# Strassen's seven products for the GLA values of a hybrid attention block

## The chip, the cores and the metric

The kernel runs on one core of one Trainium2 chip. The time is device microseconds of one execution, from its start to its last store. TensorE multiplies, VectorE and ScalarE do the elementwise work, GpSimd helps and issues some DMAs, SyncE issues most of the others.

## The reference

One layer of an encoder block on x (1 × 512 tokens × 2048, float32). What matters here:

```python
mod = silu(c) @ w_cond + b_cond
shift, scale, gate = split(mod, 3)
h = rms_norm(x) * (1 + scale) + shift
aq, ak, av, ag, gq, gk, gv, gg, lr_f, lr_b = split(h @ w_in)   # 1024 x4, 512, 512, 1024, 1024, 16, 16
a_out = dilated_attention(aq, ak, av) * silu(ag)               # 16 heads of 64, 3 patterns
log_g = log_sigmoid(lr @ gla_gate_up + bias) / 16              # forward and backward
g_out = rms_norm(gla(gq, gk, gv, log_g_f) + gla_backward(...)) * gain * silu(gg)   # 4 heads
y = concat(a_out, g_out) @ w_out
return rms_norm(x + gate * y) * final_gain
```

`gv = h @ W` is a product of 512 tokens × 2048 by 2048 × 1024. It is needed by all four GLA heads.

## The kernel before

**Precision.** Each float32 operand is split into a high part (ScalarE rounds it, `split_hi`) and the rest (VectorE subtracts, `split_lo`); a product is three matmuls, high by high, low by high and high by low (`three`, L217 to L219). `h_hi` and `h_lo` hold h transposed, 16 tiles of 128 features by 512 tokens.

**Units.** After the conditioning sums and two first units, the projection goes through units of 512 output columns: `qk2`, `qk4`, `qk6`, `gk`, `gv0`, `gv1`, `ag0`, `ag1`, `gg0`, `gg1`. A unit reads 8 weight groups of 512 KB (two tiles of 128 × 512), and each group takes 24 matmuls into four PSUM tiles. `fetch` loads a group on SyncE's queue, some groups ahead, into a pool of four buffers (`RAW`); the high and low parts have three buffers each. Then the output projection follows as two pairs of column blocks, each by Strassen's seven products (`OUT_ORDER`): four groups of 12 matmuls a product, `O0` to `O55`. Sums of weight blocks for it (T1 to T4) are made in memory by copies and accumulating DMAs on GpSimd's queue (`paced`, L393), spread over the units by `SUM_OPS_IN`; its sums of `cat` (S1 to S4) are made by VectorE.

**Side work.** A unit takes a list of (share, function): at that share of its ticks the function's instructions are issued. In the units `qk2` to `gk` this is the attention of 16 heads, four a unit: scores `s` by TensorE, an exponential `p` with its sum (VectorE and ScalarE, L736 and L739), a reciprocal (L740), a multiply by GpSimd (L744), transposes `t` (L756), an addition into `pt` (L761) and the product `o` (L770). In `gv1`, `ag0`, `ag1` and `gg0` it is one GLA head each, `gla_head`: gate logits `z` for two directions (`z00`, `z01` for head 0), then on ScalarE and VectorE their log-sigmoid `g`, its running sum `b`, a shifted copy `bm`, and the decayed `ki` and `qi`; TensorE transposes `ki` (`kt00`, `kt01`), multiplies with the values (`kv`), and so on. `SUMS_IN` spreads conditioning sums (`rawv`, `rawg`, VectorE, L316) over the units.

**The values.** `gv0` and `gv1` are such units with h as the stationary and the weights as the moving operand, so that the tokens lie on the partitions of the result. The low-rank gate input `plr` (32 matmuls) lies in `gv0`; between the two units it is stacked (`lrst`), the gate's up-projection `ups` is loaded and split; GLA head 0 starts at a fifth of `gv1` (`GLA_FIRST`).

**What sets the order.** TensorE's instructions stay in the order in which the program writes them. The other engines' are ordered by a scheduler's priorities; `urgent` raises those of side work, `issue_after(last["lo"])` puts an operation behind the last low split in VectorE's order, and `paced` ties a DMA to the last high split.

## Time and profile before

| | |
|---|---|
| median of three runs | 930.07 us (929.69 to 930.33) |
| profiled execution | 930.08 us, span 928.3 us |
| TensorE busy | 914.6 us (99%), granted clock 1.0 in every stage but the last (0.96) |
| VectorE, ScalarE, GpSimd busy | 654.9, 472.1, 100.7 us |
| DMA | 210.84 MB, mean 227 GB/s |

The stages by TensorE's time, read off the timeline:

| stage | us from the start |
|---|---|
| conditioning and first units | 0 to 188 |
| qk2, qk4, qk6, gk, with the attention | 188, 255, 321, 387 to 453 |
| gv0, with the low-rank matmuls | 453.3 to 507 |
| gv1, with GLA head 0 | 507 to 559.7 |
| ag0, ag1, gg0 with heads 1 to 3, gg1 | 559.7, 613, 667, 721 to 772 |
| output projection and tail | 772 to 928 |

In a row of the timeline the first two numbers are start and duration in us; square brackets hold the idle time of the engine before it and what ended that. A row of the table of windows gives the busy time of each engine between two times, the number of instructions in brackets, then the granted clock, the share of the DMA engines and GB/s. Matmuls overlap, so the distance of two starts, and not the duration, tells what one costs.

### The profile page before, as it was taken

The numbers are of one execution on the slowest core, as the hardware profiler recorded it, in microseconds if no ns is written. First come the engines' busy times: TensorE is split into PE (matmuls) and PEld (weight loads), VectorE is DVE, ScalarE is ACT, GpSimd is POOL, SyncE is SP. The second block draws the span as 40 slices with busy tenths as digits, with TensorE's granted clock in tenths as the row PEclk, the third lists the DMA queues.
The fourth block names the chain that finished last, engine by engine and source line by source line (L and its number), as shares of the span: only waits on it lengthen the run. The fifth ranks groups of instructions, "written<-read, shape, count | busy, mean of one in ns | idle before, by whom it ended". The sixth has DMA issues, their size and how long they took to land.

```text
span 928.3 us, 12115 instructions
## 1 busy us (share of the span) xinstructions
PE 914.6 (99%) x4375; PEld 759.6 (82%) x4375; DVE 654.9 (71%) x960; ACT 472.1 (51%) x770; POOL 100.7 (11%) x152
## 2 busy tenths in 40 slices
PE   8999999999999999999999999999999999999995
PEld 6888788888888888888877888888888888888884
DVE  7988799866665766767544747576696539697496
ACT  5553533565654655655513545364553338455564
POOL 0000000012212223122000110101021000000001
PEclk9999999999999999999999999999999999999998
DMA  9999497564765775655665647668686667856743
GB/s 347 403 414 387 161 378 294 182 210 134 193 198 156 208 237 155 219 167 172 186 235 192 187 137 243 199 203 252 210 266 193 207 176 269 315 183 230 280 171 136
DMA packets 54629, 210.84 MB, mean 227 GB/s; under 512 B 7237, under 2 KB 7525, under 8 KB 46249
## 3 DMA queue, kind: packets, MB, share of 16 engines
q1 hardware_dynamic: 48946, 175.89, 51.9%
q0 software_dynamic: 5184, 33.62, 15.4%
q8 instruction: 34, 0.56, 0.2%
q10 hardware_dynamic: 440, 0.57, 0.2%
q14 instruction: 25, 0.20, 0.1%
HBM read 201.57 MB, written 37.84 MB: 258 GB/s over the span
## 4 chain that ended last, share of the span: by engine, by line
PE 92%; DVE 3%; ACT 2%; DMA 1%; issue 1%; SPq 0%; DVEq 0%; ACTq 0%
PE ps_qk L217 5%; PE ps_qk L219 5%; PE ps_qk L218 5%; PE g L219 4%; PE g L217 4%; PE g L218 4%; PE o L770 3%; PE ps_gv L219 3%; PE ps_gv L218 3%; PE stb L219 3%; PE ps_gv L217 3%; PE stb L217 3%; PE stb L218 3%; PE t L756 3%; PE ps_ag L217 3%; PE ps_ag L219 3%
## 5 line engine op out<-in xcount | busy, mean ns | idle before, releaser
L316 DVE CUSTOM_DVE_ANT_0 cb<-cb,sb,c_bcond 128x2048 f32<-128x2048 f32 (+1 forms) x32 | 73.4, 2295 | 1.6 <-DMA cb<-in_wm 1.2
L739 ACT ACTIVATE p<-p,st 128x512 f32<-128x512 f32 x64 | 46.1, 721 | 53.1 <-DVE st L736 52.6
L393 POOL DMA_DIRECT2D T<-in_w_o x48 | 33.5, 704 | 305.5 <-ACT qk21h L444 119.8
L744 POOL TENSOR_SCALAR p<-p,st 128x512 f32<-128x512 f32 x62 | 44.6, 719 | 194.7 <-DVE st L740 141.5
L736 DVE CUSTOM_DVE_ANT_0 p<-s,g 128x512 f32<-128x512 f32 x64 | 43.7, 687 | 18.0 <-PE s L733 17.7
L761 DVE TENSOR_TENSOR pt<-t,pt 128x512 fp32r<-128x512 f32 x64 | 43.7, 688 | 15.0 <-ACT pt L760 14.7
L760 ACT ACTIVATE pt<-t 128x512 fp32r<-128x512 f32 x64 | 37.8, 591 | 11.1 <-PE t L756 10.0
L756 PEld LDWEIGHTS t<-c_ident,p 128*128 128x128 f32 x256 | 31.5, 140 | 9.7 <-POOL p L744 1.4
L756 PE MATMUL t<-c_ident,p 128*128 128x128 f32 x256 | 38.5, 273 | 0.1
L770 PEld LDWEIGHTS o<-pt,vv 128*128 128x128 f32 x256 | 34.8, 188 | 2.8
L770 PE MATMUL o<-pt,vv 128*128 128x256 f32 x256 | 35.6, 281 | 0.0
L740 DVE RECIPROCAL st<-st 128x1 f32<-128x1 f32 x64 | 10.3, 161 | 24.5 <-ACT p L739 24.4
L733 PE MATMUL s<-kl,qs 128*128 128x512 f32 x64 | 25.0, 391 | 0.0
L732 PE MATMUL s<-ks,qs 128*128 128x512 f32 x64 | 25.0, 390 | 0.0
L945 ACT ACTIVATE sq<-st,sc 128x256 f32<-128x256 f32 x24 | 12.2, 507 | 19.7 <-DVE st L935 10.5
L777 DVE TENSOR_TENSOR cat<-o,oh 64x256 f32<-64x256 f32 x32 | 13.3, 417 | 11.1 <-ACT oh L773 10.7
L1273 POOL TENSOR_SCALAR x<-x,rn 128x512 f32<-128x512 f32 x3 | 3.4, 1132 | 158.4 <-ACT rn L1262 158.4
L316 DVE CUSTOM_DVE_ANT_0 rawg<-rawg,crow,c_bcond 128x1024 f32<-128x1024 f32 x16 | 20.4, 1279 | 0.0
L316 DVE CUSTOM_DVE_ANT_0 rawg<-rawg,crow,gate 128x1024 f32<-128x1024 f32 x16 | 20.2, 1278 | 0.2 <-DMA rawg<-in_wg 0.2
L773 ACT ACTIVATE oh<-o 64x256 f32<-64x256 f32 x32 | 12.2, 381 | 15.0 <-PE o L770 14.0
L508 ACT ACTIVATE h_hi<-xt,shift 128x512 fp32r<-128x512 f32 x16 | 11.5, 719 | 12.8 <-DVE shift L316 12.8
L977 PE MATMUL go<-qi,sq 128*128 128x128 f32 x96 | 15.9, 275 | 0.0
(1520 smaller groups left out, 2968.1 us busy)
## 6 DMA issues: line engine op xcount, KB each, us to landing
cb<-in_wm SPq DMA_DIRECT2D x31, 1024.0 KB, 8.5
T<-in_w_o POOLq DMA_DIRECT2D x48, 512.0 KB, 5.2
rawg<-in_wg SPq DMA_DIRECT2D x32, 512.0 KB, 4.8
raw_O<-T SPq DMA_DIRECT2D x32, 512.0 KB, 4.5
raw_qk<-in_w_qk SPq DMA_DIRECT2D x24, 512.0 KB, 3.4
raw_O<-in_w_o SPq DMA_DIRECT2D x24, 512.0 KB, 3.3
rawb<-in_w_sb SPq DMA_DIRECT2D x16, 512.0 KB, 5.3
rawv<-in_wv SPq DMA_DIRECT2D x16, 512.0 KB, 3.4
```

Source lines behind the costliest of these rows:

```text
L217: mm(ps, lh, rh, start=first, stop=False, skip_group_check=more)
L218: mm(ps, ll, rh, start=False, stop=False, skip_group_check=more)
L219: mm(ps, lh, rl, start=False, stop=last, skip_group_check=more)
L316: nc.vector.tensor_tensor_reduce(out=w, in0=w, in1=with_, op0=ALU.mult, op1=ALU.add, scale=1.0, scalar=init, accum_out=dst)
L393: move = nc.gpsimd.dma_start(dst, src, max_dma_last_dim=8192, **how).ins
L736: nc.vector.tensor_tensor_reduce(out=t, in0=ps, in1=gt[h][:, P * i:P * i + 512], op0=ALU.add, op1=ALU.min, scale=1.0, scalar=3e38, accum_o ...
L739: act(t, t, AF.Exp, bias=st[:, 0:1], scale=-1.0, accum_out=st[:, 1:2])
L744: last["pool"] = nc.gpsimd.tensor_scalar(t, t, st[:, 2:3], 1.0, op0=ALU.mult, op1=ALU.mult).ins
L756: nc.tensor.transpose(pk[:, kt * P:kt * P + P], t[:, kt * P:kt * P + P], ident)
L760: act(hi, src, AF.Copy)
L761: tt(lo, src, hi.bitcast(F32), op=ALU.subtract)
L770: mm(po[:, :256], vv[h // 4][:, kt, h % 4, :], t[:, w, kt, :], start=kt == 0 and w == 0, stop=kt == 3 and w == 1)
```

## The change

`gv0` and `gv1` become one unit `V` of seven products (`VAL_ORDER`), in blocks of 256 tokens and 1024 features by 1024 features and 512 columns. Each product has four groups of 12 matmuls, `V0` to `V27`: 336 instead of 384.

- Its token sums S1 to S4 are made by VectorE in the units qk2, qk4, qk6 and gk (`token_sums`: three operations on 128 × 512 at 0.3 of the unit's ticks, seven at 0.75), stored to memory on SyncE's queue in pieces of 256 KB, loaded again in `V` (eight loads of 512 KB) and split there (`vS...`).
- Its weight sums T1 to T4 are made in memory on GpSimd's queue, 32 operations. The output projection's T1 no longer is (16 operations less): its two blocks are loaded (`raw_O`, `raw_P`) and added by VectorE (L471).
- P2, P4, P5 and P3 are merged into `gv0` and `gv1` by VectorE (L1280, L1282 and others) as their PSUM is read.
- In `V` the low-rank matmuls come at ticks 10 to 40, the gate's preparation (`up_load`, `up_split`, `lr_stack`) is side work, and GLA head 0 gets shares of its own (`GLA_FIRST`).
- Conditioning sums move out of the value units: `SUMS_IN` gives qk4 5, qk6 5, gk 6, ag0 8, ag1 8, gg0 9, and the rest (7) fall to gg1.

```diff
 GLA_AT = (0.01, 0.02, 0.33, 0.46, 0.46, 0.56, 0.64, 0.76, 0.76, 0.88)
-GLA_FIRST = 0.2
-
-SUMS_IN = {"qk6": 4, "gk": 4, "gv0": 9, "gv1": 3, "ag0": 7, "ag1": 8, "gg0": 9}
+GLA_FIRST = (0.42, 0.45, 0.6, 0.66, 0.75, 0.79, 0.84, 0.9, 0.92, 0.97)
+
+SUMS_IN = {"qk4": 5, "qk6": 5, "gk": 6, "ag0": 8, "ag1": 8, "gg0": 9}
 
 
 OUT_ORDER = ("P1", "P7", "P6", "P4", "P5", "P3", "P2")
 OUT_PAIRS = ((0, 1), (3, 2))
-OUT_WEIGHTS = {"P1": "11", "P7": "T3", "P6": "T2", "P4": "T4", "P5": "T1", "P3": "22", "P2": "21"}
-OUT_SUMS = {"T1": ("11", "12"), "T3": ("12", "22"), "T2": ("T1", "22"), "T4": ("T2", "21")}
+VAL_ORDER = ("P1", "P7", "P6", "P4", "P2", "P5", "P3")
+WEIGHTS = {"P1": "11", "P7": "T3", "P6": "T2", "P4": "T4", "P5": "T1", "P3": "22", "P2": "21"}
+BLOCK_SUMS = {"T3": ("12", "22"), "T2": ("T3", "11"), "T4": ("T2", "21"), "T1": ("11", "12")}
 OUT_DEEP = 6
-SUM_OPS_IN = {"qk2": 9, "qk4": 9, "qk6": 6, "gk": 6, "gv0": 4, "gv1": 5, "ag0": 7, "ag1": 7, "gg0": 6, "gg1": 5}
+SUM_OPS_IN = {"qk2": 11, "qk4": 11, "qk6": 10, "gk": 9, "V": 6, "ag0": 9, "ag1": 8, "gg0": 8, "gg1": 8}
...
-    order = ["qk2", "qk4", "qk6", "gk", "gv0", "gv1", "ag0", "ag1", "gg0", "gg1"]
-    groups = [(u, g) for u in order for g in range(KT // 2)]
+    groups = [(u, g) for u in ("qk2", "qk4", "qk6", "gk") for g in range(KT // 2)]
+    groups += [("V", s) for s in range(4 * len(VAL_ORDER))]
+    groups += [(u, g) for u in ("ag0", "ag1", "gg0", "gg1") for g in range(KT // 2)]
     groups += [("O", s) for s in range(2 * 4 * len(OUT_ORDER))]
...
+            elif u == "V":
+                raws[i] = val_fetch(g)
...
+    second = {}
+
+    def out_fetch(s):
+
+        pair, q = divmod(s, 4 * len(OUT_ORDER))
+        what, g = WEIGHTS[OUT_ORDER[q // 4]], q % 4
+        t = out_tile(s, f"raw_O{s}")
+        if what == "T1":
+            block_load(t, pair, "11", g)
+            second[gi["O", s]] = block_load(out_tile(s + 1, f"raw_P{s}"), pair, "12", g)
+            return t
+        return block_load(t, pair, what, g)
+
+    def val_fetch(s):
+
+        what, g = WEIGHTS[VAL_ORDER[s // 4]], s % 4
+        if s % 3 and (s % 3 == 1 or s < 22):
+            t = two.tile([P, 2, 512], F32, tag=" hl"[s % 3], name=f"raw_V{s}")
+        else:
+            t = RAW(f"raw_V{s}", [2, 512])
+        return block_load(t, "V", what, g)
...
-    sum_ops = []
-    for s in range(13):
-        for lag, fn, name in ((0, sum_start, "T1"), (0, sum_start, "T3"), (1, sum_add, "T1"), (1, sum_add, "T3"),
-                              (2, sum_start, "T2"), (3, sum_add, "T2"), (4, sum_start, "T4"), (5, sum_add, "T4")):
-            if 0 <= s - lag < 8:
-                sum_ops.append(fn(*[((s - lag) // 4), name, (s - lag) % 4]))
+    def steps(keys, names):
+        r = []
+        for s in range(len(keys) + 5):
+            for lag, name in enumerate(names):
+                for fn, q in ((sum_start, s - 2 * lag), (sum_add, s - 2 * lag - 1)):
+                    if 0 <= q < len(keys):
+                        r.append(fn(keys[q][0], name, keys[q][1]))
+        return r
+
+    sum_ops = steps([("V", g) for g in range(4)], ("T3", "T2", "T4"))
+    for q, (fn, g) in enumerate((fn, g) for fn in (sum_start, sum_add) for g in range(4)):
+        sum_ops.insert(3 * q + 1, fn("V", "T1", g))
+    sum_ops += steps([(pair, g) for pair in range(2) for g in range(4)], ("T3", "T2", "T4"))
...
             raw = raws[i].rearrange("p k c -> p (k c)")
+            if i in second:
+                tt(raw, raw, second[i].rearrange("p k c -> p (k c)"), op=ALU.add)
...
-        at = GLA_AT
-        if h == 0:
-            at = [GLA_FIRST + (1 - GLA_FIRST) * x for x in at]
+        at = GLA_AT if h else GLA_FIRST
...
+    def minus_a21(n, th, kh, kp):
+        t, t3 = pair_tile(f"{n}{kp}")
+        e, e3 = pair_tile(f"{n}e{kp}")
+        tt(t3, h_part(h_hi, th, kh, kp), h_part(h_hi, 1, 0, kp), op=ALU.subtract)
+        tt(e3, h_part(h_lo, th, kh, kp), h_part(h_lo, 1, 0, kp), op=ALU.subtract)
+        tt(t, t, e, op=ALU.add)
+        s_store(n, kp, t)
+        return t3
+
+    def token_sums(kp):
+
+        def s3():
+            with tc.issue_after(last["lo"]):
+                minus_a21("S3", 0, 0, kp)
+
+        def rest():
+            with tc.issue_after(last["lo"]):
+                s1 = minus_a21("S1", 1, 1, kp)
+                t2, t23 = pair_tile(f"S2{kp}")
+                stt(t23, s1, -1.0, h_part(h_hi, 0, 0, kp), op0=ALU.mult, op1=ALU.subtract)
+                tt(t23, t23, h_part(h_lo, 0, 0, kp), op=ALU.subtract)
+                s_store("S2", kp, t2)
+                t4, t43 = pair_tile(f"S4{kp}")
+                tt(t43, t23, h_part(h_hi, 0, 1, kp), op=ALU.add)
+                tt(t43, t43, h_part(h_lo, 0, 1, kp), op=ALU.add)
+                s_store("S4", kp, t4)
+        return [(0.3, s3), (0.75, rest)]
...
-        ps = unit(n, False, attention((p, p + 1)) + ([(0.05, shift_row)] + some_sums(n) if p == 4 else []))
+        ps = unit(n, False, attention((p, p + 1)) + token_sums(p // 2)
+                  + ([(0.05, shift_row)] if p == 2 else []) + (some_sums(n) if p else []))
         for q in range(2):
             qk_evict(p + 2 + q, ps[2 * q], ps[2 * q + 1])
 
-    ps = unit("gk", False, attention((6, 7)) + [(0.5, lambda: cond_half(0))] + some_sums("gk"))
+    ps = unit("gk", False, attention((6, 7)) + token_sums(3) + some_sums("gk"))
...
-    ps = unit("gv0", True, some_sums("gv0"), lr=lr_tick)
...
-    ps = unit("gv1", True, gla_head(0) + some_sums("gv1"))
...
+    tokens = {"P1": h_view(0, 0), "P4": h_view(1, 1), "P2": h_view(0, 1),
+              "P7": s_view("S3"), "P6": s_view("S2"), "P5": s_view("S1"), "P3": s_view("S4")}
+
+    def values_unit(side):
+        n_groups = 4 * len(VAL_ORDER)
+        for p, n in enumerate(VAL_ORDER):
+            if n in ("P7", "P6", "P5", "P3"):
+                name = {"P7": "S3", "P6": "S2", "P5": "S1", "P3": "S4"}[n]
+                for z in range(2):
+                    q = 4 * p + 2 * z
+                    side.append((max(q - 5, 0.1) / n_groups, s_load(name, z)))
+                    side.append(((q - 1.9) / n_groups, s_parts(name, z)))
+        side = sorted([(x * 4 / 7, go) for x, go in spill] + side + block_sums("V"), key=lambda x: x[0])
...
+        pos, tick, ticks = 0, 0, 4 * n_groups
+        v0, chains, p7 = gla["v0"], {}, []
+        first_of = {"P1": "g1", "P7": "gx", "P2": "g2", "P3": "g3"}
+        chain_of = {"P1": "g1", "P6": "g1", "P5": "g1", "P7": "gx", "P4": "gx", "P2": "g2", "P3": "g3"}
+        for p, n in enumerate(VAL_ORDER):
+            c_ = chain_of[n]
+            if n in first_of:
+                chains[c_] = [PJ(f"ps_gv_{n}{r}") for r in range(2)]
+            ps = chains[c_]
+            for g in range(4):
+                i0 = gi["V", 4 * p + g]
+                split_hi(i0)
+                split_hi(i0 + 1)
+                for ahead in (2, 3, 4, 5):
+                    fetch(i0 + ahead)
+                split_lo(i0)
+                wh, wl = wts[i0]
+                for r in range(2):
+                    for kk in range(2):
+                        k = 2 * g + kk
+                        ah, al = tokens[n](k, slice(P * r, P * r + P))
+                        cw = slice(512 * kk, 512 * kk + 512)
+                        three(ps[r], ah, al, wh[:, cw], wl[:, cw], n in first_of and k == 0, k == 7,
+                              n not in first_of)
+                        tick += 1
+                        if tick >= 10 and tick % 2 == 0 and tick < 42:
+                            low_rank((tick - 10) // 2)
...
+                    if r == 0:
+                        split_lo(i0 + 1)
+            for r in range(2):
+                if n == "P1":
+                    act(v0[:, r, :], ps[r], AF.Copy)
+                elif n == "P7":
+                    p7.append(T2(f"p7{r}"))
+                    act(p7[r], ps[r], AF.Copy)
+                elif n == "P6":
+                    act(v0[:, 2 + r, :], ps[r], AF.Copy)
+                elif n == "P4":
+                    tt(v0[:, 2 + r, :], ps[r], v0[:, 2 + r, :], op=ALU.add)
+                elif n == "P2":
+                    tt(v0[:, r, :], ps[r], v0[:, r, :], op=ALU.add)
+                elif n == "P5":
+                    if r == 0:
+                        gla["v1"] = B8("gv1", [4, 512])
+                    act(gla["v1"][:, r, :], ps[r], AF.Copy)
+                    stt(gla["v1"][:, 2 + r, :], ps[r], -1.0, p7[r], op0=ALU.mult, op1=ALU.subtract)
+                else:
+                    tt(gla["v1"][:, r, :], ps[r], gla["v1"][:, r, :], op=ALU.subtract)
...
+    values_unit([(0.1, up_load), (0.3, up_split), (0.385, lr_stack), (0.93, lambda: cond_half(0))] + gla_head(0))
```

VectorE's order around the gates of GLA head 0, from the second direction's log-sigmoid on: `g`, `b`, `bm`, `ki`, `qi` are those of the text above, `gv15l` and `V18l` are low parts of weight groups, `rawg` is a conditioning sum, `vS` the low part of a token sum. Before:

```order
L430 TENSOR_TENSOR gv15l<-raw_gv_4664,gv15h 128x1024
L316 ISA rawg_4541,gate_1493<-rawg_4541,crow_3831,c_bcond 128x1024
L316 ISA gate_1493 128x1
L884 TENSOR_TENSOR g_4606<-g_4606,e_4602 128x512
L891 SCALAR_TENSOR_TENSOR b_4609<-rst,g_4606 128x512
L900 TENSOR_TENSOR bm_4614<-b_4609 128x512
L906 TENSOR_TENSOR ki_4618<-ki_4618,gkt 128x512
L907 TENSOR_TENSOR qi_4617<-qi_4617,gqt 128x512
```

And after:

```order
L918 TENSOR_TENSOR g_4660<-g_4660,e_4656 128x512
L462 TENSOR_TENSOR V18l<-raw_V_4683,V18h 128x1024
L925 SCALAR_TENSOR_TENSOR b_4663<-rst,g_4660 128x512
L462 TENSOR_TENSOR V19l<-raw_V_4701,V19h 128x1024
L934 TENSOR_TENSOR bm_4668<-b_4663 128x512
L1215 TENSOR_TENSOR vS_4905<-rawS_4813,vS_4905 128x1024
L462 TENSOR_TENSOR V20l<-raw_V_4721,V20h 128x1024
L940 TENSOR_TENSOR ki_4672<-ki_4672,gkt 128x512
L941 TENSOR_TENSOR qi_4671<-qi_4671,gqt 128x512
```

The four steps g, b, bm and ki, which stood together, now have three low parts of weights and one of a token sum between them.

VectorE's order in the output projection from the end of P6 to the middle of P5: `O12l` to `O20l` are low parts, `y` and `x` the merging of finished columns. Before:

```order
L430 TENSOR_TENSOR O13l<-raw_O_6746,O13h 128x1024
L430 TENSOR_TENSOR O14l<-raw_O_6766,O14h 128x1024
L430 TENSOR_TENSOR O15l<-raw_O_6787,O15h 128x1024
L430 TENSOR_TENSOR O16l<-raw_O_6807,O16h 128x1024
L430 TENSOR_TENSOR O17l<-raw_O_6832,O17h 128x1024
L1246 TENSOR_TENSOR y_6917<-gx_6661,u_6825 128x512
```

And after, with the additions of T1's two blocks (L471):

```order
L471 TENSOR_TENSOR raw_O_6993<-raw_O_6993,raw_P_6995 128x1024
L462 TENSOR_TENSOR O13l<-raw_O_6932,O13h 128x1024
L462 TENSOR_TENSOR O14l<-raw_O_6952,O14h 128x1024
L471 TENSOR_TENSOR raw_O_7020<-raw_O_7020,raw_P_7022 128x1024
L462 TENSOR_TENSOR O15l<-raw_O_6973,O15h 128x1024
L471 TENSOR_TENSOR raw_O_7042<-raw_O_7042,raw_P_7044 128x1024
L462 TENSOR_TENSOR O16l<-raw_O_6993,O16h 128x1024
L471 TENSOR_TENSOR raw_O_7064<-raw_O_7064,raw_P_7066 128x1024
L1413 TENSOR_TENSOR y_7112<-gx_6847,u_7013 128x512
L462 TENSOR_TENSOR O17l<-raw_O_7020,O17h 128x1024
```

Each addition stands ahead of the low parts that the next product needs, the fourth ahead of the first merge.

VectorE's order at the second batch of token sums, in `qk4`: `S1e` and `S_...` are the sums, `p` and `st` the exponential's input and its sum, `cat` the attention's output. Before:

```order
L736 ISA p_2604,st_2605<-s_2601,g_2383 128x512
L736 ISA st_2605 128x1
L740 RECIPROCAL st_2605<-st_2605 128x1
L761 TENSOR_TENSOR pt_2566<-t_2613,pt_2566 128x4x128
L736 ISA p_2626,st_2627<-s_2623,g_2526 128x512
```

And after:

```order
L770 ISA p_2685,st_2686<-s_2682,g_2581 128x512
L770 ISA st_2686 128x1
L1113 TENSOR_TENSOR S_2721<-h_hi 128x512
L1114 TENSOR_TENSOR S1e_2722<-h_lo 128x512
L774 RECIPROCAL st_2686<-st_2686 128x1
L1115 TENSOR_TENSOR S_2721<-S_2721,S1e_2722 128x512
L795 TENSOR_TENSOR pt_2697<-t_2698,pt_2697 128x4x128
L1129 SCALAR_TENSOR_TENSOR S_2727<-S_2721,h_hi 128x512
L811 TENSOR_TENSOR cat_1592<-o_2709,oh_2718 64x256
L1130 TENSOR_TENSOR S_2727<-S_2727,h_lo 128x512
L462 TENSOR_TENSOR qk60l<-raw_qk_2738,qk60h 128x1024
```

Two sums now stand between an exponential's sum and its reciprocal, and one ahead of each of the two operations that follow.

129 lines of the change are left out of this document (81 added, 48 removed).

## The prediction

> **What bounds the kernel now.** I read the page's first part, then TensorE's list of waits, then the table of windows, and only then groups, chain and timeline. In this order, a row or more of each of the first three:
>
> ```profile
> PE 914.6 (99%) x4375; PEld 759.6 (82%) x4375; DVE 654.9 (71%) x960; ACT 472.1 (51%) x770; POOL 100.7 (11%) x152
> PE warm L283 <- DVE hot L295: 1.5, 1, 1.5
> core 0: us, PE busy (x) PEld busy (x) DVE busy (x) ACT busy (x) POOL busy (x), PEclk, DMA share, GB/s
> 255.00:321.00 66.00, 65.98 (x352) 55.54 (x351) 41.70 (x88) 37.10 (x73) 16.17 (x25) 1.00 0.64 185
> 321.00:387.00 66.00, 65.99 (x353) 55.44 (x352) 45.39 (x97) 37.21 (x73) 15.58 (x22) 1.00 0.66 204
> ...
> 453.00:507.00 54.00, 54.00 (x241) 42.71 (x241) 21.51 (x28) 13.70 (x17) 2.61 (x4) 1.00 0.61 202
> 507.00:559.00 52.00, 52.00 (x263) 44.14 (x262) 32.88 (x43) 25.34 (x44) 5.33 (x9) 1.00 0.55 160
> ...
> 772.00:850.00 78.00, 77.86 (x344) 64.51 (x344) 67.26 (x76) 46.93 (x61) 0.00 (x0) 1.00 0.71 257
> ```
>
> TensorE is busy for the whole of every stage shown, and its longest wait of the run is 1.5 us, at the start. So a matmul that is left out is time won, and any lateness of another engine that reaches TensorE is time lost, one for one. The stages differ in cover: beside the value units (453 to 559) VectorE works 21.5 of 54 and 32.9 of 52 us, beside the attention 42 to 45 of 66, and in the output stage 67.3 of 78. The profiled run took 930.08 us, 1.78 us more than its span of 928.3 and 0.01 from the median of 930.07, so I sum against 930.08.
>
> **The matmuls that go.** Two value units of 192 matmuls (8 weight groups of 24) become 7 products of 4 groups of 12, 336: 48 fewer. The price is the interval at which such matmuls follow one another, not the 0.39 us of one row, since they overlap:
>
> ```profile
> 801.75 0.39 PE L217 MATMUL gx<-O13h,c_h 128*128 128x512 f32 x1
> ...
> 812.63 0.39 PE L217 MATMUL g<-O17h,c_h 128*128 128x512 f32 x1
> ```
>
> O13 to O16 are four groups of the output stage in the same shape as the new products: 48 matmuls in 812.63 − 801.75 = 10.88 us, 0.227 each. The 48 that go are worth **−10.9 us**. The low-rank matmuls and GLA head 0 stay, in other places.
>
> **Token sums beside the attention (units qk2, qk4, qk6, gk).** Each unit gets 10 VectorE operations on 128x512; the nearest rows (one of the groups by line, then the timeline) are
>
> ```profile
> L1239 DVE TENSOR_TENSOR y<-y,gate_b 128x512 f32<-128x512 f32 x16 | 10.6, 685 | 0.1
> 269.76 0.15 DVE L740 RECIPROCAL st<-st 128x1 f32<-128x1 f32 x1
> 270.08 0.69 POOL L744 TENSOR_SCALAR p<-p,st 128x512 f32<-128x512 f32 x1 [3.22 <-DVE st L740]
> 272.59 0.60 PE L756 MATMUL t<-c_ident,p 128*128 128x128 f32 x4
> 525.21 1.28 DVE L316 CUSTOM_DVE_ANT_0 rawg<-rawg,crow,c_bcond 128x1024 f32<-128x1024 f32 x1
> ```
>
> so 10 × 0.685 = 6.9 us a unit, and up to 5 conditioning sums of 1.28 us more (qk4, which had none). VectorE goes from 41.7 to about 55 of 66 us in qk4. The seven operations of the second batch are the danger: they stand among the reciprocals and the `pt` additions of the attention, three or four of them ahead of one reciprocal or `pt`, which is then 2 to 3 us late. What covers it is the distance at which TensorE uses a result: here the reciprocal ends at 269.91, GpSimd's multiply at 270.77, and the transposes come at 272.59, 1.8 us later. I take 0.1 us a unit, **+0.5** in all with the four stores a unit on SyncE's queue (the weight loads behind them have two groups, over 10 us, in hand); the ends are 0 (all within cover) and 3 us late less 1.8, that is 1.2 a unit, 4.8.
>
> **The sums of weights in memory** go from 64 to 80 issues on GpSimd's queue:
>
> ```profile
> L393 POOL DMA_DIRECT2D T<-in_w_o x48 | 33.5, 704 | 305.5 <-ACT qk21h L444 119.8
> T<-in_w_o POOLq DMA_DIRECT2D x48, 512.0 KB, 5.2
> raw_O<-T SPq DMA_DIRECT2D x32, 512.0 KB, 4.5
> ```
>
> 16 × 0.70 = 11 us of an engine that is busy 16 of 66 us beside the attention; nearly all stand where its multiplies leave gaps (3.22 us in the row above). I cost them at nothing; were one in four to push a multiply past its 1.8 us of cover, 4 × 0.7 = 2.8 us would show.
>
> **The new value unit.** Its groups need VectorE and ScalarE twice as often: 28 weight splits in 336 × 0.227 = 76 us of products, instead of 16 in 106 us, and 8 splits of token sums. VectorE: 36 × 1.22 = 44 us in place of 16 × 1.22 = 20, less 12 conditioning sums (15 us): 54.4 + 24 − 15 = 63 of about 95 us. That is cover on the average, so I looked for one place where the order leaves none. It is the second transposition of GLA head 0 (`kt01`). The same chain before, `z` and `kt` from the chain that ended last, the rest from the timeline:
>
> ```profile
> 515.24 0.45 PE z L877 x2
> 519.43 1.20 DVE L430 TENSOR_TENSOR gv14l<-raw_gv,gv14h 128x1024 fp32r<-128x1024 f32 x1
> ...
> 524.07 1.22 DVE L430 TENSOR_TENSOR gv15l<-raw_gv,gv15h 128x1024 fp32r<-128x1024 f32 x1
> ...
> 529.88 0.69 DVE L906 TENSOR_TENSOR ki<-ki,gkt 128x512 f32<-128x512 f32 x1 [0.80 <-ACT ki L904]
> 530.64 1.04 ACT L444 ACTIVATE gv16h<-raw_gv 128x1024 fp32r<-128x1024 f32 x1
> 531.71 0.33 PE kt L916 x3
> ```
>
> From `z00` (515.24) to the end of `ki01` (530.57) it took 15.3 us with 3.7 us of unrelated VectorE work in it (`gv14l`, `gv15l`, one conditioning sum), and `kt` came 1.1 us after. In the new order three 128x1024 splits and one token split stand between `g01` and `ki01` alone, and some 10.4 us of unrelated work in the whole chain: 15.3 + 6.7 = 22 us. TensorE meanwhile has 82 matmuls to do between `z00` and `kt01`, 82 × 0.227 = 18.6: it would wait 3.4 us. A second count is smaller: `V20h` can be made only when V17's high half has been used, and `V20l` and `ki01` follow it, 1.04 + 1.22 + 0.69 and the steps between them, about 3.3 us, against 8 matmuls, 1.8 us: 1.5 us. I take 2.5, nearer the first because it is the whole chain (ends 1.5 and 5, the second if two more splits of 1.22 fall due late). Beside it the gate's input (`lr_stack`, moved into the unit) about 0.5, the second PSUM row of P2, which waits for the eviction of P7's row on VectorE (one 0.69 us operation), 0.7, the end of the head 0.3: **+4.0** (1 to 7).
>
> **T1 in the output stage.** It is no longer read as a sum, but as two blocks that VectorE adds: 4 additions of 1.22 and 4 more loads in each of the two pairs.
>
> ```profile
> 800.10 1.23 DVE L430 TENSOR_TENSOR O14l<-raw_O,O14h 128x1024 fp32r<-128x1024 f32 x1 [1.49 <-ACT O14h L444]
> ...
> 808.26 1.23 DVE L430 TENSOR_TENSOR O17l<-raw_O,O17h 128x1024 fp32r<-128x1024 f32 x1 [1.49 <-DMA raw_O<-in_w_o]
> ...
> 813.13 1.22 DVE L430 TENSOR_TENSOR O18l<-raw_O,O18h 128x1024 fp32r<-128x1024 f32 x1
> ...
> 815.81 0.39 PE L219 MATMUL g<-O18l,c_h 128*128 128x512 f32 x1
> ```
>
> Four gaps of 1.49 us stand ahead of O14l to O17l, and each new addition is 1.22. They would all fit, but the fourth (for O19) needs loads that start only once O14l and O15l have freed their buffers, 4.5 us earlier, so it falls behind 808.26, where VectorE has no gap until O20l. `O18l` ended at 814.35 and is used at 815.81: 1.46 us of cover against 1.22 and a late start of under 1 us. I take 0.5 a pair, **+1.0**; the ends are 0 and 2 a pair (the third addition late too), 4.
>
> **Sum.** 930.08 − 10.9 + 0.5 + 4.0 + 1.0 = 924.7, against the median **924.6 us**.
>
> [...] Among the attention's rows these two run side by side:
>
> ```profile
> 288.61 0.69 POOL L744 TENSOR_SCALAR p<-p,st 128x512 f32<-128x512 f32 x1 [2.34 <-DVE st L740]
> 288.60 0.69 DVE L761 TENSOR_TENSOR pt<-t,pt 128x512 fp32r<-128x512 f32 x1 [0.16 <-ACT pt L760]
> ```
>
> Neither is longer than its usual 0.69. But `t` lies in PSUM there, and the token sums have both inputs in SBUF; no row of this profile shows such an operation beside a multiply of GpSimd. [...]
>
> **The rivals.**
> 1. All covers hold: 930.08 − 10.9 = 919.2, with at most 1 us of waits, 919 to 920.5. For it: VectorE idles over 30% of the value stage. Against it: the two counts of the `kt01` chain. 0.15.
> 2. Late everywhere, a little: the upper ends of two of the three terms, +7 and +4 instead of +4 and +1: 930.6 with the attention at 0.5, no change that can be told. 0.11.
> 3. [...] 0.13.
> 4. The value unit's loads don't keep up and every group is late: 0.4 us × 28 = 11 us, 932. DMA engines were 0.55 to 0.61 busy there and get 36 loads in 95 us instead of 16 in 106. 0.04; it would be slower too.
>
> **How the numbers follow.** The forecast, 921 to 928, has 0.57. A measurement of this kernel tells 0.2%, 1.9 us. Faster by more than that: the forecast and rival 1, and a third of rival 2, 0.75. Within it: most of rival 2 and a part of rival 3, 0.10. Slower: the rest, 0.15. The range takes in the covers held, 919.0, and reaches up to rival 4, 932.0; rival 3's larger half and the worst combinations stay outside.
>
> **What would show it.** In the new profile: 336 matmuls of the value products, and that unit about 95 us plus 4 of waits; one wait of TensorE of 1.5 to 5 us at `kt01`, released by VectorE's `ki01`; waits under 1 us at the start of P2's second row and around O18l and O46l; attention units of 66 to 66.5 us. The forecast is wrong if an attention unit takes over 67.5 us, if the products follow one another at more than 0.227 us over whole groups (loads or splits late), or if a token sum or a multiply is recorded or spaced far over 0.69 us.

## The result, and the profile after

The changed kernel takes **936.17 us** (median of 5 runs, 934.48 to 937.54) against 930.07: 1.0062 of the time before, with a 95% interval of 1.0044 to 1.0081. The forecast was 924.6, with a range of 919.0 to 932.0. The profiled run took 937.23 us, its span is 935.5.

The first part of the page and TensorE's list of waits (in all, times, longest), answering to those of before:

```profile
PE 909.5 (97%) x4327; PEld 751.9 (80%) x4327; DVE 710.3 (76%) x1036; ACT 491.8 (53%) x790; POOL 120.6 (13%) x168
PE kt L950 <- DVE ki L940: 3.1, 1, 3.1
PE s L766 <- DVE pt L795: 2.2, 1, 2.2
PE g L220 <- DVE O55l L462: 1.8, 1, 1.8
PE t L790 <- POOL p L778: 1.7, 2, 0.9
...
PE s L766 <- DMA ks<-ks: 0.9, 1, 0.9
...
PE ps_gv_P L218 <- DVE gv L1280: 0.6, 1, 0.6
PE g L220 <- DVE O46l L462: 0.5, 1, 0.5
```

Before, nothing behind the start made TensorE wait over 1 us. Now there is a wait of about 2 or 3 us in each of three regions: the attention (`s`), the value unit (`kt`) and the tail (`O55l`). The table of windows, cut where each stage's first matmul starts (`qk4`, `qk6`, `gk`, the value unit in two parts, the tail), in the columns of before:

```profile
253.66:323.60 69.94, 66.81 (x354) 55.78 (x353) 51.72 (x109) 36.78 (x71) 21.45 (x27) 1.00 0.86 253
323.60:391.29 67.69, 66.61 (x354) 55.77 (x352) 53.27 (x111) 38.94 (x74) 20.88 (x26) 1.00 0.82 231
391.29:459.12 67.83, 66.84 (x354) 55.75 (x353) 48.91 (x103) 37.24 (x71) 17.67 (x22) 1.00 0.78 232
459.12:511.00 51.88, 51.40 (x228) 40.26 (x227) 32.41 (x32) 31.17 (x41) 2.11 (x3) 1.00 0.75 246
511.00:561.30 50.30, 46.61 (x229) 38.84 (x229) 34.50 (x43) 27.83 (x43) 4.28 (x8) 0.97 0.63 199
...
915.00:935.50 20.50, 8.92 (x32) 6.54 (x30) 9.86 (x19) 6.45 (x16) 1.26 (x1) 0.74 0.29 107
```

The granted clock in the last two rows is below 1.0, which the forecast did not have in it. Measured in the same way in both traces, from a stage's first matmul to the next stage's:

| us | before | after | difference | forecast |
|---|---|---|---|---|
| qk2 | 65.37 | 65.35 | 0.0 | |
| qk4, qk6, gk | 66.33, 66.50, 66.34 | 69.94, 67.69, 67.83 | +6.3 | +0.5 (four units) |
| value products | 106.38 | 102.18 | −4.2 (−10.9 and +6.7) | −6.9 (−10.9 and +4.0) |
| ag0 to gg1 | 206.15 | 206.16 | 0.0 | 0 |
| output stage, to O55 | 146.11 | 147.62 | +1.5 | +1.0 |
| O55 to the end | 16.39 | 20.39 | +4.0 | 0 |
| before qk2 | 188.73 | 188.31 | −0.4 | 0 |

The differences add up to 7.2 us, which is that of the spans (935.5 − 928.3). By first matmuls, as here, `gv1` of the kernel before starts at 505.6 us, `gg1` at 722.3 and the output projection at 765.8; the table of stages of the kernel before has 507, 721 and 772. The three losses, one by one:

**The attention.** In `qk4` VectorE and then TensorE, from the timeline, and from the chain of waits the two transfers ahead of them:

```profile
270.49 1.23 DVE L885 CUSTOM_DVE_ANT_0 rawv<-rawv,shb 128x1024 f32<-128x1024 f32 x1 [3.12 <-DMA shb<-srow]
...
273.57 0.50 PE L766 MATMUL s<-ks,qs 128*128 128x512 f32 x1 [2.24 <-DVE pt L795]
```

```profile
259.84 5.99 DMA srow<-shiftt
265.88 4.47 DMA shb<-srow
```

The first conditioning sum (`rawv`) stands in VectorE's order ahead of a `pt` that the scores need, and it waits 3.12 us for the broadcast of the shift row. `pt` stands behind it there and starts at 272.85, and `s` at 273.57. In `qk6` and `gk` it is GpSimd that comes late (0.90 and 0.84 us), and in `gk` a load of `ks` too (0.9). GpSimd's rows in `qk6`, with VectorE's beside them:

```profile
305.23 0.69 DVE L1115 TENSOR_TENSOR S<-S,S1e 128x512 f32<-128x512 f32 x1
305.43 1.06 POOL L778 TENSOR_SCALAR p<-p,st 128x512 f32<-128x512 f32 x1 [1.55 <-PE ps_qk L220]
...
316.81 1.27 DVE L317 CUSTOM_DVE_ANT_0 rawv<-rawv,shb,vbias 128x1024 f32<-128x1024 f32 x1
317.05 1.59 POOL L778 TENSOR_SCALAR p<-p,st 128x512 f32<-128x512 f32 x1 [2.10 <-PE ps_qk L220]
318.69 0.66 PE L790 MATMUL t<-c_ident,p 128*128 128x128 f32 x4 [0.90 <-POOL p L778]
```

A multiply, 0.70 us in the median of the 62, takes 1.06 us here beside a token sum and 1.59 beside a conditioning sum. In both cases it ends about 0.56 us after VectorE's instruction has ended (305.92 and 306.49, 318.08 and 318.64). Only the second of these reaches TensorE.

**The value unit.** Transposition `kt01` on TensorE, VectorE's steps ahead of it, then the granted clock of the microseconds behind it:

```profile
520.52 0.39 PE L220 MATMUL ps_gv_P<-V18l,h_hi 128*128 128x512 f32 x1
523.98 0.55 PE L950 MATMUL kt<-c_ident,ki 128*128 128x128 f32 x3 [3.07 <-DVE ki L940]
```

```profile
519.25 1.20 DVE L462 TENSOR_TENSOR V19l<-raw_V,V19h 128x1024 fp32r<-128x1024 f32 x1
520.36 0.69 DVE L934 TENSOR_TENSOR bm<-b 128x512 f32<-128x512 f32 x1
520.96 1.22 DVE L1215 TENSOR_TENSOR vS<-rawS,vS 128x1024 fp32r<-128x1024 f32 x1
522.10 1.22 DVE L462 TENSOR_TENSOR V20l<-raw_V,V20h 128x1024 fp32r<-128x1024 f32 x1
523.23 0.69 DVE L940 TENSOR_TENSOR ki<-ki,gkt 128x512 f32<-128x512 f32 x1
```

```profile
524.00:525.00 1.00, 1.00 (x6) 0.91 (x7) 0.52 (x1) 0.44 (x1) 0.00 (x0) 1.00 0.88 242
525.00:526.00 1.00, 1.00 (x4) 0.77 (x4) 0.00 (x0) 0.14 (x2) 0.00 (x0) 0.69 0.83 315
526.00:527.00 1.00, 1.00 (x4) 0.78 (x3) 0.00 (x0) 0.97 (x1) 0.00 (x0) 0.50 0.90 340
```

VectorE runs without a gap in the order that the prediction showed, and TensorE waits for it. Then TensorE runs for 3.4 us at half the clock (0.43 us a matmul instead of 0.227), which is another 1.6 us.

**The tail.** `O55l`, the last low part of all, of before and then of after:

```profile
911.03 1.22 DVE L430 TENSOR_TENSOR O55l<-raw_O,O55h 128x1024 fp32r<-128x1024 f32 x1
...
912.37 0.44 PE L219 MATMUL g<-O55l,A12h 128*128 128x512 f32 x1
```

```profile
914.41 0.68 DVE L1406 TENSOR_TENSOR y<-y,gate_b 128x512 f32<-128x512 f32 x1
...
915.01 1.28 DVE L1407 TENSOR_TENSOR x<-y,x 128x512 f32<-128x512 f32 x2
...
916.21 1.22 DVE L462 TENSOR_TENSOR O55l<-raw_O,O55h 128x1024 fp32r<-128x1024 f32 x1
...
917.48 0.50 PE L220 MATMUL g<-O55l,A12h 128*128 128x512 f32 x1 [1.80 <-DVE O55l L462]
```

Before, it ended at 912.25 and was used at 912.37: 0.12 us of slack. Behind T1's additions VectorE is later there, and its order puts more merging (`y`, `x`) ahead of `O55l`: 1.80 us of wait, and 3.4 us of half clock again behind it, from 917.91 on.

### The profile page after: what moved, and what is told of

It reads as the page before. It is cut to its first block, busy times and chain, and to the rows that moved or that the text cites. A ratio compares the mean times of both kernels' runs of the same rounds, so it can differ in the third digit from the quotient of the medians.

```text
span 935.5 us, 12266 instructions
## 1 busy us (share of the span) xinstructions
PE 909.5 (97%) x4327; PEld 751.9 (80%) x4327; DVE 710.3 (76%) x1036; ACT 491.8 (53%) x790; POOL 120.6 (13%) x168
## 2 busy tenths in 40 slices
DMA packets 62247, 238.13 MB, mean 255 GB/s; under 512 B 8197, under 2 KB 8485, under 8 KB 52841
## 4 chain that ended last, share of the span: by engine, by line
PE 80%; DVE 7%; DMA 7%; ACT 3%; issue 2%; POOL 0%; SPq 0%; DVEq 0%; ACTq 0%; POOLq 0%
PE ps_qk L218 4%; PE ps_qk L220 4%; PE ps_qk L219 4%; PE g L220 3%; PE stb L220 3%; PE stb L218 3%; PE stb L219 3%; PE g L219 3%; PE g L218 3%; PE ps_ag L218 3%; PE ps_ag L220 3%; PE ps_ag L219 3%; PE o L804 3%; PE t L790 3%; PE sta L219 2%; PE sta L220 2%
## 5 line engine op out<-in xcount | busy, mean ns | idle before, releaser
L778 POOL TENSOR_SCALAR p<-p,st 128x512 f32<-128x512 f32 x62 | 53.7, 866 | 177.1 <-DVE st L774 125.7
L418 POOL DMA_DIRECT2D T<-in_w_o x32 | 23.4, 731 | 166.7 <-ACT V12h L478 17.4
L418 POOL DMA_DIRECT2D T3V<-in_w_gv x8 | 5.3, 661 | 119.8 <-ACT qk21h L478 119.8
L418 POOL DMA_DIRECT2D T<-T x16 | 8.9, 558 | 76.0 <-ACT V17h L478 17.5
```

What stands on the lines that cost most here:

```text
L418: move = nc.gpsimd.dma_start(dst, src, max_dma_last_dim=8192, **how).ins
L778: last["pool"] = nc.gpsimd.tensor_scalar(t, t, st[:, 2:3], 1.0, op0=ALU.mult, op1=ALU.mult).ins
```

## The experiments

Ratios are to the kernel before, run on the same chip (about 929.8 us). Diffs are against the changed kernel unless another is named. Times of stages and waits are those of the one profiled execution, which can lie some microseconds from the median: 930.04 in run 3, 940.48 in run 5, 935.31 in run 8, 926.65 in `room_and_evict_early`.

**1. T1 of the output projection in memory again.**

```diff
-SUM_OPS_IN = {..., "V": 6, "ag0": 9, "ag1": 8, "gg0": 8, "gg1": 8}
+SUM_OPS_IN = {..., "V": 6, "ag0": 13, "ag1": 12, "gg0": 12, "gg1": 12}
-        if what == "T1":
-            ...
+    sum_ops += steps([(pair, g) for pair in range(2) for g in range(4)], ("T1",))
```

> The changed kernel, except that the output projection's T1 is again summed in memory (16 more operations on GpSimd's queue, 80 to 96, spread over ag0 to gg1) and VectorE adds no blocks there. Theory: the 3.16 - 1.65 = 1.5 us that pair 1 lost, the 1.8 us wait for O55l and the half clock after it (about 1.7 us) come from VectorE being behind because of the additions; the order at O55l is the old one again. Then the output stage and the tail come within 0.5 us of before, and the time is 936.2 - 5.2 = 931, 930.5 to 932. Rival: the tail is late because the whole program is later in another phase of the clock or the loads; then 935 to 937.

934.70 us, 1.0052 [1.0040, 1.0064]. The output projection from O0 on took 162.7 us (before 162.5, changed 168.0) without a wait over 0.2 us: its 5.5 us come from T1's additions. But only 1.5 of them arrive in the total. `qk4` took 71.4 and the value unit 104.2 (half clock behind waits of 2.2, 1.7 and 2.5 us), `ag0` 1.6 more, with the DMA engines at 0.87 to 0.91 in `ag0` to `gg0`, where most of the 16 more sums of weights stand.

**2. The shift row a unit earlier.**

```diff
-                  + ([(0.05, shift_row)] if p == 2 else []) + ...
+                  + ([(0.05, shift_row)] if p == 0 else []) + ...
```

> The changed kernel, with the transposition and broadcast of the shift row (shift_row: two small DMAs) issued at 0.05 of qk2 instead of qk4. Theory: in qk4 VectorE stood 3.1 us at the first conditioning sum, which waited for the broadcast, and TensorE 2.2 us behind it; with the row there in time this goes: qk4 takes 66.5 to 67.5 us instead of 69.9 and the time is about 933.5 (932.5 to 934.5). Rival: it is the added work on VectorE (51.7 of 69.9 us) that is late in qk4; then qk4 stays at 69 to 70 us and the time at 935 to 937.

940.0 us, 1.0111 [1.0098, 1.0124]. `qk4` fell to 67.2 as expected, and `qk2` rose by 3.1 to 68.5, with three waits of 0.8 to 1.0 us: the loss had moved with the row. The time rose by 3.8 us all the same. In the trace the value unit took 1.9 more (a wait of 1.8 at `V14h`), `gg0` 1.4 more and the output projection's first pair 1.8 more, and why a shift row that comes earlier should do this stays open.

**3. `kt01` later.** GLA head 0's fourth share from 0.66 to 0.71, 5.6 of the unit's 112 ticks.

> The changed kernel, with the second transposition of GLA head 0 at 0.71 of the value unit's ticks instead of 0.66 (five ticks, 15 matmuls, 3.4 us later), VectorE's order unchanged. Theory: the 3.1 us wait for ki01 goes, and with it the 3.3 us at half clock behind it (1.6 us); the value unit takes 97.5 us instead of 102.2 and the time is about 931.5 (930.5 to 933). Rival: only the wait goes and the clock falls all the same, or the next step (kv) waits in its place: 933 to 936.

933.07 us, 1.0037 [1.0024, 1.0050]. The wait at `kt` and the half clock are gone together, the value unit takes 98.3 us, 3.9 less than in the changed kernel; the median fell by 3.1. The wait of `kt01` was what the prediction said, and its price was higher by the clock.

**4. No arithmetic in the token sums.** `token_sums` stores parts of `h_hi` in place of sums.

> The changed kernel without the arithmetic of the token sums: the four stores a unit take parts of h as they are, so the values are those of other operands; all DMAs stay. Theory: of the time that qk6 and gk lost (1.2 and 1.5 us) most is GpSimd's multiplies, 0.69 us alone and 0.95 to 1.07 where a token sum ran beside them, together with VectorE's 6.9 us a unit; without the sums qk6 and gk take 66.5 to 67 us, no multiply in qk2 is longer than 0.75, and the time is about 934 (933 to 935.5). Rival: the loss is in the DMAs (0.78 to 0.86 busy instead of 0.61 to 0.66): then qk6 and gk stay at 67.7 and 67.8 us and the time at 936.

936.99 us, 1.0076 [1.0054, 1.0098]. The attention's losses stay, unit by unit (69.6, 67.7, 67.2), at the same waits:

```profile
PE s L766 <- DVE pt L795: 2.0, 1, 2.0
PE t L790 <- POOL p L778: 1.7, 2, 0.9
```

The token sums do not cause them.

**5. The last low parts ahead of the merges.** `O54l` and `O55l` get a higher priority.

> The changed kernel, with the low parts of the last two weight groups raised in VectorE's priority: O55l stands before both additions to x and one multiplication by the gate, three operations of about 0.6 us earlier. T1 stays on VectorE. Theory: the tail is long only because O55l is late; the 1.6 to 1.8 us wait and the half clock behind it go, the tail from O55 on takes 16.5 us instead of 18.6 to 20.4, and the time is 936.2 - 3 = 933 (932 to 934.5). Rival: the additions that now stand behind O55l end later and the chain of the last norm takes the time back: 935 to 937.

936.14 us, 1.0073 [1.0059, 1.0088]. No wait at `O55l`, 2.5 us less from O55 to the end; in this profile `V14h` (1.4) and `O18l` (1.6) were later than in the changed kernel's, and V had 6.8 us of half clock at `kt`. Nothing is left in the total, and no run separates this gain from those losses.

**6. Conditioning sums back out of the attention.**

```diff
-SUMS_IN = {"qk4": 5, "qk6": 5, "gk": 6, "ag0": 8, "ag1": 8, "gg0": 9}
+SUMS_IN = {"qk4": 0, "qk6": 4, "gk": 4, "ag0": 9, "ag1": 10, "gg0": 10}
```

> The changed kernel, with the conditioning sums (1.28 us each on VectorE, both inputs in SBUF) taken out of qk4 and partly out of qk6 and gk: 0, 4, 4 instead of 5, 5, 6 there, and ag0, ag1, gg0, gg1 take 9, 10, 10, 11 instead of 8, 8, 9, 7. The token sums stay. Theory: what the attention units lost (3.6, 1.2, 1.5) is VectorE at the first conditioning sum, waiting for the shift row, and GpSimd's multiplies beside later ones (1.6 us instead of 0.69, TensorE 0.9 us behind them, twice). Then qk4 takes 66.3 to 67, qk6 and gk 66.5 to 67.2, and the time is 936.2 - 4.5 = 931.7 (930.5 to 933.5). Rival: the token sums take the place of the conditioning sums, or gg1 with 11 sums is late by as much: 935 to 938.

937.97 us, 1.0082 [1.0069, 1.0095]. The attention units are whole again, with every token sum in them:

```profile
253.40:319.90 66.50, 66.49 (x355) 55.82 (x354) 46.77 (x99) 37.71 (x74) 18.71 (x27) 1.00 0.80 223
319.90:386.20 66.30, 66.29 (x354) 55.81 (x353) 51.28 (x106) 37.08 (x71) 19.99 (x26) 1.00 0.82 228
386.20:452.60 66.40, 66.37 (x354) 55.70 (x353) 48.20 (x102) 36.91 (x72) 16.83 (x22) 1.00 0.77 227
```

6.2 us come back there, and `ag0`, `ag1` and `gg0`, which got the sums, lose 1.6, 2.3 and 3.8: `kt` of their GLA heads waits 2.05 and 2.26, `kv` 1.1.

**7. Runs 1, 3 and 6 together.**

> The changed kernel with three things together: T1 summed in memory, kt01 at 0.71, and the conditioning sums moved as in cond_sums_back. Theory: the three losses stand in different places and add up: 936.2 - 5.2 - 4 - 4.5 = 922.5 (921 to 925), faster than before by 0.5 to 1%. Rival: the 32 more sums in memory than before and the value unit's loads slow one another (the wait for V14h, 0 to 1.8 us in the runs so far, and half clock behind it): 925 to 929.

935.82 us, 1.0069 [1.0044, 1.0095]. The attention (66.5, 66.4, and 67.9 with a late load of `ks`) and V (98.3) are mended, `ag0` takes 61.7 and the output projection's first pair 82.0 instead of 76.8 (wait of 3.8 at `O2l`). The loss has a new place again.

**8. The kernel before, with only the conditioning sums moved** as the change moves them, and the shift row, which they need, with them from `qk6` to `qk4`:

```diff
-SUMS_IN = {"qk6": 4, "gk": 4, "gv0": 9, "gv1": 3, "ag0": 7, "ag1": 8, "gg0": 9}
+SUMS_IN = {"qk4": 5, "qk6": 5, "gk": 6, "gv0": 0, "gv1": 0, "ag0": 8, "ag1": 8, "gg0": 9}
...
-        ps = unit(n, False, attention((p, p + 1)) + ([(0.05, shift_row)] + some_sums(n) if p == 4 else []))
+        ps = unit(n, False, attention((p, p + 1)) + ([(0.05, shift_row)] if p == 2 else []) + (some_sums(n) if p else []))
```

> The kernel before, without any of the new products, but with its conditioning sums and the shift row placed as in the changed kernel: 5, 5, 6 in qk4, qk6, gk, none in gv0 and gv1, then 8, 8, 9 and 7. Theory: the sums alone cost the attention units most of what they lost: qk4 68 to 70 us instead of 66.3, qk6 and gk 67 to 67.8, the time 930 + 4 = 934 (932 to 936). Rival: the sums are harmless without the token sums and the 80 operations in memory: 929.5 to 931.

938.65 us, 1.0089 [1.0075, 1.0103], without a product or a token sum changed: 8.8 us in the median, more than the whole change lost. The profiled execution, the shortest of the five, shows 5.2 of it. `qk4` took 69.4, `qk6` 67.7 and `gk` 66.9 us, 4.8 more in all, and `gg0` 1.5 more. Its waits are those of the changed kernel's attention:

```profile
PE t L756 <- POOL p L744: 1.7, 2, 0.9
PE s L732 <- DVE pt L761: 1.6, 1, 1.6
```

The value units took 106.38 us, to the hundredth as before: the 12 sums had cost nothing there. They were put out of a place that was free, eight of them into the attention, one into `ag0` and three into `gg1`.

**9 to 13. Other places for the sums.** All start from run 1 with `kt01` later, `qk4` without conditioning sums and `qk6` and `gk` with four each. `room_in_v_early` puts six into the first 0.4 of V and ten sums of weights beside it; `room_and_evict_early` also raises the merging of P4; `room_in_gg1` leaves V without and gives 16 to `gg1`. `first_sum_later` delays the first conditioning sum of `ag0`, `ag1` and `gg0` in `room_and_evict_early` by a slot, and `first_sum_and_spread` moves sums of weights forward besides. (All but `room_in_gg1` also load the later `rawv` into the pool `RAW`.)

> The changed kernel with T1 summed in memory, kt01 at 0.71, and the conditioning sums where VectorE has room: none in qk4, 4 in qk6, 4 in gk, 6 in the first 0.4 of the value unit (before GLA head 0's gates), 7, 8, 9 in ag0, ag1, gg0 as in the kernel before, 10 in gg1. Theory: three_mended lost 14 us in ag0 to gg0 and at the start of the output stage because the sums that left the attention stood beside GLA heads 1 to 3; without that the units ag0 to gg0 take 54.1, 54.1, 54.4 again, the attention units 66.4, the value unit 98.5, and the time is 930 - 8 = 922 (920.5 to 925). Rival: the value unit has no room for the sums and loses what the others win: 926 to 931.

> As room_in_v_early, and the two additions of P4 into gv0 are raised in VectorE's priority, so that they stand ahead of V17l: TensorE waited 0.6 to 1.3 us there for the second PSUM row of P2. Theory: this wait goes, 0.5 to 1.3 us less than room_in_v_early (921, 919.5 to 924). Rival: the step falls due elsewhere (V17l, kt01) and the time is that of room_in_v_early.

> As room_in_v_early, but with no conditioning sum in the value unit: gg1 takes 16. Theory: with 16 x 1.28 = 20 us more in gg1's 43.5 us of matmuls VectorE is late at the start of the output stage (O2l, as in three_mended, 3.8 us) : 925 to 928. Rival: gg1 has the room and this is the best place: 920.5 to 923.

> As room_and_evict_early, and the first conditioning sum of ag0, ag1 and gg0 comes one place later (with the second), so that its load has 13 us instead of 5.4. Theory: in ag0 VectorE stood 5.0 us at that sum, waiting for its load with the DMA engines 0.92 busy, and kt01 of head 1 (1.8 us and half clock) fell behind it, the same in gg0; then ag0 and gg0 take 54.1 and 54.4 us instead of 56.1 and 56.4 and the time is 929.7 - 3 = 926.5 (925 to 928). Rival: two sums in a row fall due beside the gates' chain and kt01 waits for them: 929 to 931.

> As first_sum_later, and the 96 sums in memory are spread by 13, 13, 12, 11 over qk2 to gk, 14 in the value unit, 8, 8, 8, 9 after it, instead of 11, 11, 10, 9, 10, 13, 13, 12, 7. Theory: the DMA engines, 0.91 to 0.95 busy in ag0 to gg0, come down to about 0.8 there, and what still waits for loads goes: 924.5 (922.5 to 926.5). Rival: the value unit, which takes its weights by 36 loads, is late instead (V14h): 927 to 930.

Measured, in this order: 932.89 us (1.0033 [1.0020, 1.0045]), 929.71 (1.0004 [0.9989, 1.0020], 12 runs from 926.65 to 934.63), 935.76 (1.0073 [1.0053, 1.0094]), 933.23 (1.0038 [1.0026, 1.0051]) and 937.02 (1.0081 [1.0067, 1.0095]). The best is not to be told from the kernel before. Its profile, of the shortest of the 12 runs, shows where the conditioning sums hang now, in VectorE's row and in the DMA share (the second figure from the end) of `ag0`, `ag1` and `gg0`:

```profile
560.43 1.23 DVE L882 CUSTOM_DVE_ANT_0 rawv<-rawv,shb 128x1024 f32<-128x1024 f32 x1 [5.00 <-DMA rawv<-in_wv]
```

```profile
552.00:606.00 54.00, 52.19 (x262) 44.05 (x261) 34.99 (x49) 23.00 (x39) 10.60 (x17) 1.00 0.92 275
606.00:660.00 54.00, 54.00 (x272) 45.81 (x271) 37.51 (x53) 26.95 (x45) 10.53 (x17) 1.00 0.95 282
660.00:713.00 53.00, 50.91 (x257) 43.03 (x256) 43.46 (x59) 27.55 (x45) 11.25 (x14) 1.00 0.92 294
```

VectorE stands 5.00 us before a sum whose weights have not landed, and the gates of GLA head 1 stand behind it; `kt` of that head then makes TensorE wait 1.8 us. In the kernel before the share was 0.68 to 0.75 there. Delaying the first sum mended `ag0` (54.1) and broke `gg0` (61.6, a wait of 5.1 at `kt`); with the sums of weights moved forward as well, the value unit took 109.5 us.

**14 and 15. Half of the sums of weights.** The accumulating half is left out, 40 of 80 in the changed kernel and 48 of 96 in `room_and_evict_early`; everything that reads them stays.

```diff
-            paced(dsum[pair, name, g], flat(block(pair, BLOCK_SUMS[name][1], g)), accum_op=ALU.add)
+            pass
```

> The changed kernel without the accumulating half of its sums in memory (40 of 80 operations; the copies stay), so that the sums hold their first block only. All else, VectorE's order too, is that of the changed kernel. Theory: what it lost is VectorE's order (conditioning sums beside the attention, ki01, T1's additions) and not the DMA load; the attention units, the value unit and the tail stay long, 934 to 936. Rival: the DMA load (0.75 to 0.86 busy) makes the shift row, the scores' rows and the weights late; without these operations qk4 takes under 68 us and the time is 930 to 932.

> As room_and_evict_early (three places mended, 96 sums in memory), without the accumulating half of the sums in memory (48 of 96). Theory: in that kernel the loads are what is left: the DMA engines fall from 0.91 to 0.95 to about 0.8 in ag0 to gg0, the first conditioning sum of a unit no longer waits 5 us for its load, kt01 of heads 1 and 3 is in time, and the time is 929.7 - 5 = 924.5 (922.5 to 927). Rival: VectorE's order alone keeps heads 1 and 3 late: 928.5 to 931.

931.41 us (1.0021 [1.0010, 1.0032]) and **919.52** (0.9891 [0.9878, 0.9905], 919.39 to 920.24). The same three windows of the second, and its list of waits behind the start, entire:

```profile
552.00:606.00 54.00, 54.00 (x272) 45.80 (x271) 37.82 (x53) 25.20 (x42) 4.46 (x9) 1.00 0.65 220
606.00:660.00 54.00, 54.00 (x271) 45.84 (x270) 37.60 (x52) 27.46 (x46) 4.96 (x10) 1.00 0.64 214
660.00:713.00 53.00, 52.87 (x266) 44.62 (x265) 43.90 (x60) 28.43 (x47) 7.70 (x10) 1.00 0.67 229
```

```profile
PE ps_gv_P L219 <- DVE vS L1212: 0.9, 1, 0.9
PE ps_gv_P L218 <- DVE gv L1278: 0.2, 1, 0.2
```

In the first the rival's range came true: `s` in `qk4` waits 0.2 us in place of 2.2, and `qk4` takes 67.9, `gk` 66.8 and V 99.7 us, while the multiplies of `qk6` and the waits at `kt` (2.6) and `O55l` (2.0) stay. In the second, with the load gone, TensorE is full: V takes 97.3 us, 9.1 less than the two units of before, and the sum `rawv` that waited 5.00 us for its load waits 0.61. The time is what rival 1 gave for covers that all hold. These sums cost the changed kernel 4.8 us and the mended one 10.2. Leaving them out takes away their transfers and their issues on GpSimd together; for the transfers speaks that the multiplies stayed as long as they were (mean 866 and 864 ns in the changed kernel, 791 and 792 in the other), while the loads landed sooner (`rawv` 5.0 to 3.3 us, 5.3 to 3.9 in the median). A run with the issues and without the transfers was not made.

**16 and 17. Every sum made, but fewer in memory.** `room_and_evict_early` with T1 by VectorE for one pair (88 sums) and for both (80, with run 5's priority).

> The mended kernel with the evictions early (room_and_evict_early, 96 memory sums, 929.71 us), but T1 of the output projection's first pair added by VectorE from its two blocks, T1 of the second pair still summed in memory: 88 memory sums. If DMA load is what holds it, each memory sum is worth about 0.2 us (96 gave 929.7, 48 gave 919.5), less the two extra loads: about 927.5 to 928.5. If the loss lies in where the conditioning sums stand and not in the load, there is no change, 929 to 931. If VectorE's additions in the first pair cost what the changed kernel showed there (0.2 to 0.8), it stays within these.

> As the run beside it, but T1 of both pairs added by VectorE, 80 memory sums as in the changed kernel, and the last two low parts of the output projection raised so that they are not behind the merges. By the load: 926 to 928. By the place of the conditioning sums: 929 to 932. If the late low part at the tail comes back in another place, 2 to 4 us more.

937.00 us (1.0074 [1.0062, 1.0087]) and 931.08 (1.0017 [1.0006, 1.0028]). Fewer sums did not help: `kt` in `gg0` waits 4.4 and 2.2 us, in the first with half clock behind it. The total load alone does not order these runs. That it also matters where a late load meets VectorE's order is a reading of the waits, not shown by a run of its own. A version that leaves all twelve sums in the value unit was not run, and that a complete version beats the kernel before was not shown.

## Why the prediction was wrong, point by point

Two steps failed: the token-sum term, which priced the sums and not what had to make room for them, and the sums of weights, which were put at nothing. The value unit had the right waits at too low a price, and T1 brought one wait, at `O55l`, that no term held.

**Matmuls, −10.9: right.** 48 fewer (4375 to 4327), at 0.227 in the undisturbed groups (519.62, 519.84, 520.07, the starts of V18's; 2.72 us for the twelve of V13). With the load gone and one wait of 0.9, 9.1 of it was seen.

**Token sums, +0.5: right for them, wrong for the units.** Run 6 has them at +0.06 over three units. The term failed by what it left out: the conditioning sums that the change moves in entered only as VectorE's busy time ("up to 5 conditioning sums of 1.28 us more"). Neither the load that the first waits for nor the multiply that takes 1.59 us beside such a sum of 1.27 was priced. Measured +6.3; run 8 shows 4.8 of it without the rest of the change, and run 6 takes it away.

**Rival 3** (0.13) put a high price, my estimate, on token sums beside GpSimd's multiplies. No run shows that price: without the sums' arithmetic (run 4) the attention's losses stay. What the trace shows in its place is the multiply going from 0.69 us to 1.06 beside a token sum and to 1.59 beside a conditioning sum, and ending 0.56 us after the VectorE instruction. The prediction says that no row of the profile before shows an operation with both inputs in SBUF beside a multiply; two do, and this is one of them:

```profile
354.86 1.21 DVE L851 CUSTOM_DVE_ANT_0 rawv<-rawv,shb 128x1024 f32<-128x1024 f32 x1
...
355.11 1.52 POOL L744 TENSOR_SCALAR p<-p,st 128x512 f32<-128x512 f32 x1 [2.34 <-DVE st L740]
```

So the price of a conditioning sum beside a multiply, 0.83 us, could have been read before the change (the other is at 421.44). There the transposes came 1.56 us after the multiply's end, so nothing reached TensorE. All 62 multiplies had a mean of 719 ns before, 796 without token sums, 795 without most conditioning sums and 866 with both; but not every multiply has the cover of 1.8 us that I read off one of them. The one at 317.05 would have ended at 317.74 alone and was due at 318.69 − 0.90 = 317.79: 0.05. Of the 6.3 us, 1.7 are two such waits (0.90 and 0.84); 2.2 are the wait behind the shift row and 0.9 a load of `ks`; the rest lies in no wait over 0.3 us and stays open.

**Sums of weights, "I cost them at nothing": the second step that failed.** I asked whether their issues push GpSimd's multiplies and never whether their bytes delay loads. 238.13 MB instead of 210.84 moved, the DMA share beside the attention went from 0.64 to 0.86 in `qk4`, and half of them were worth 4.8 us. These are not beside the other terms but inside them: in the trace without that half `qk4` is 2.0 us shorter, `gk` 1.0 and the value unit 2.5, and the output stage 2.1 longer.

**The value unit, +4.0: measured +6.7.** `kt01` waited 3.1 (2.5, from 1.5 to 5), P2's second row 0.6 (0.7). Missing was half clock behind the wait, 1.6; another 0.5 is at `V14l`, and 0.9 lies in no wait over 0.1 us and stays open. Rival 4's late groups did not come, the products follow one another at 0.227; one group, V14, was 1.4 to 1.8 us late in the traces of runs 1, 2 and 5.

**T1, +1.0: +1.5 up to O55, and +4.0 behind it.** Of the output stage's small waits, that at O46 came (0.5); at O18 there was none in this trace, and 0.8 to 1.6 in those of runs 3, 4 and 5. I stopped at O19 and its repetition at O46; the place with least slack, 0.12 us at `O55l`, I had not looked for. Rival 2 came near these two terms (+7 and +4 against 6.7 and 5.5), with the attention at 0.5.

## What to carry to other kernels

When a change takes over a stage that had room, price what used that room: here 12 unrelated operations that were free before, and cost 4.8 us beside the attention (eight of them, run 8), 7.6 beside GLA heads 1 to 3 (four of them, run 6) and 8 at the start of the output stage (`room_in_gg1`, 16 in `gg1`). Spread over all places, they cost nothing that the trace shows once 48 accumulating transfers were left out (`room_half_sums`). Follow a VectorE instruction that is moved to its load and to everything queued behind it, and count the bytes added to the DMA engines against the latest load, not only the issues against an engine. And price a wait of TensorE of 1.7 us or more as the wait and a chance of half clock behind it (22 of 32 in the traces of this case).
